# Other orders of Strassen's seven products in the MLP, and one sum of weights made from another sum's tile in SBUF

## Chip, core and metric

The program runs on one core of one Trainium2 chip. The metric is the device time of one execution in microseconds (us). TensorE is called PE here, VectorE DVE, ScalarE ACT, GpSimd POOL; SP is the engine that issues most of the plain DMAs. Weight loads into PE are listed apart as PEld.

## What is computed

One layer of a hybrid backbone on 1024 latent tokens of width 1024 (with 256 context tokens): a token mixer (long convolution, linear attention and a gated delta rule side by side, an input and an output projection), then a squared-ReLU MLP with a hidden width of 4096, and a final norm. The change touches the MLP alone:

```
def sq_relu_mlp(h, w1, w2):
    return jnp.square(jax.nn.relu(h @ w1)) @ w2

x = x + g1 * y                                    # y: output projection of the mixer
x = x + g2 * sq_relu_mlp(modulate(x, norm2_g[l], sh2, sc2), w_mlp1[l], w_mlp2[l])
return rmsnorm(x, final_norm_g)
```

All of it is float32.

## The kernel before

The recurrences of the mixer end near 900 us of the trace. Behind them come nine *stages*, one after the other: the output projection, and for each of four groups g of 1024 hidden channels an up stage (`in_w1[g]`) and a down stage (`in_w2[g]`). A stage multiplies a 1024x1024 block of weights by a 1024x1024 activation with one level of Strassen's scheme: seven products of 512x512 blocks, called product 1 to product 7 here, in an order that a tuple gives (`O1`, `O2`, `O3`). The up stage of g = 0 uses O2, the other up stages and all four down stages O1.

A product is four *chunks* p = 0 to 3. A chunk is 12 matmuls 128x512 into one bank of PSUM: four slices k of the contraction, each in three matmuls, because every float32 operand is split into two fp32r parts (`mm3`: hi x hi, hi x lo, lo x hi). So a product is 48 matmuls and a stage 336.

*Weights.* A product's weights are a sum of some of the four blocks (i, j) of the stage's weights (signs are already in the stored blocks). Such a sum lies in a tile `wr` of 128x2048 (1 MB). `PLANS[order]` has five such tiles, each a list in order of time: a pair (i, j) is a block to load or to add, a number is the product that then uses the tile. The first block of a tile is a plain load that SP issues (L1489); each further one is a DMA that adds to the tile, issued by POOL (L1483). There are four rooms of SBUF for the five tiles, so a tile's first load waits until the last user of the room's former tile is done. For each chunk the weights are split: ACT copies the high part (`S<-wr`, L291), then POOL subtracts to get the low part (`S<-wr,S`, L251). There are four buffers `S`, so the split can run four chunks, one product, ahead of PE.

*Activations.* `sums` makes the four operands `T` (slice k = 0 to 3) of the next product: perhaps a sum on DVE, then ACT's copy of the high part and DVE's subtraction (`T<-ar,T` in a down stage, `T<-h,T` in an up stage). There are ten buffers `T0` to `T9`.

*Results.* Products 6, 7 and 4 are added in PSUM on top of product 1's banks, and product 3 on top of product 5's (`bank`). After each chunk `take` reads the bank: in an up stage it makes the tiles `ar` of the squared ReLU, b11 and so on for the next down stage (b11 is done with product 2, b21 with product 4, b22 with 7 or 5, b12 with 3); in a down stage DVE adds it to the residual `x`.

Each engine runs its instructions in the order that a scheduler wrote at build time; an instruction that waits for a semaphore holds up all behind it on its engine. That holds for POOL's DMA issues, too: an adding DMA waits until the tile's former load or sum has landed. The up stage of g = 0 is special: its product 6 runs with its four chunks interleaved (`together`), so it needs all four `S` at once. The last stage splits product 4 in two halves of 256 columns, so that the final norm can start earlier.

Of the kernel before, what the change touches and what calls it, by code (L numbers as in the profile page):

```python
# [14 lines left out]
ADD, SUB, MUL, MIN, MAX = ALU.add, ALU.subtract, ALU.mult, ALU.min, ALU.max  # L15
# [163 lines left out]
def steps(st):  # L179
# [20 lines left out]
NORM1_AT = (1, 1)  # L200
FINAL_AT = (4, 1)

O1, O2, O3 = (1, 5, 6, 3, 2, 7, 4), (1, 2, 6, 7, 4, 5, 3), (1, 5, 2, 6, 7, 4, 3)

PLANS = {O1: (((0, 0), 1, (1, 0), 7), ((1, 0), (1, 1), 5, (0, 0), (0, 1), 3), ((1, 0), (1, 1), (0, 0), 6), ((0, 1), 2), ((1, 1), 4)),
         O2: (((0, 0), 1, (1, 0), 7), ((0, 1), 2), ((1, 0), (1, 1), (0, 0), 6, (0, 1), 3), ((1, 1), 4), ((1, 0), (1, 1), 5)),
         O3: (((0, 0), 1, (1, 0), 7), ((1, 0), (1, 1), 5, (0, 0), 6, (0, 1), 3), ((0, 1), 2), ((1, 1), 4))}
PAIRS = (0, 0, 0, 0, 1, 1, 1, 1)


class Build:
# [1257 lines left out]
    def weights(self, src, order):  # L1469

        gp = self.nc.gpsimd
        at, todo, tiles = {}, [list(t) for t in PLANS[order]], {}
        base = 8 * self.nS
        self.nS += 1

        def further(t):

            while todo[t] and not isinstance(todo[t][0], int):  # L1480
                i, j = todo[t].pop(0)
                if t in tiles:
                    gp.dma_start(tiles[t], src[:, i, j, :], accum_op=ADD)  # L1483
                else:
                    used = base + order.index([x for x in PLANS[order][t] if isinstance(x, int)][-1])
                    room = min(self.rooms, key=self.rooms.get)
                    self.rooms[room] = used
                    tiles[t] = (self.W if room < 2 else self.M).tile([128, 2048], F32, name=f"wr{room}", bufs=1)
                    self.nc.sync.dma_start(tiles[t], src[:, i, j, :])  # L1489
            if todo[t]:  # L1490
                at[todo[t].pop(0)] = t

        def begin(n):
            for t in sorted(range(5), key=lambda t: order.index(first(t))):
                if t < len(todo) and t not in tiles and order.index(first(t)) <= n:
                    further(t)

        def first(t):
            return next(x for x in PLANS[order][t] if isinstance(x, int)) if t < len(todo) else order[0]

        def get(i, p):
            return self.operand(self.W, "S", 4, tiles[at[i]][:, 512 * p:512 * p + 512], gp)
        return get, begin, lambda i: further(at[i])

    def stage(self, src, order, moving, take, after=None, last=None, first=None, together=()):
# [79 lines left out]
    def in_place(self, h, order):  # L1585

        def moving(i, k):
            b11, b12, b21, b22 = h(k, 0), h(k, 1), h(k + 4, 0), h(k + 4, 1)
            if order == O1:

                if i == 5:
                    self.tt(b11, b11, b12, SUB)
                elif i == 6:
                    self.minus(b11, b11, b22)
                elif i == 7:
                    self.tt(b12, b22, b12, SUB)
                elif i == 4:
                    self.minus(b21, b11, b21)
                return {1: b11, 5: b11, 6: b11, 3: b22, 2: b21, 7: b12, 4: b21}[i]

            if i == 5 and order == O3:
                t = self.temp()
                self.tt(t, b11, b12, SUB)
                return t
            if i == 6:
                self.tt(b12, b22, b12, SUB)
                self.minus(b11, b12, b11)
            elif i == 4:
                self.minus(b21, b11, b21)
            elif i == 5:  # L1610
                self.minus(b12, b11, b22)
            return {1: b11, 2: b21, 3: b22, 4: b21, 5: b12, 6: b11, 7: b12}[i]
        return moving
# [129 lines left out]
    def mlp(self):  # L1743
        nc, M, x1 = self.nc, self.M, self.x1
        h = lambda k, c: self.H[k][:, 512 * c:512 * c + 512]
        for g in range(4):
            order = O1 if g else O2
            b = {}
            new = lambda: M.tile([128, 512], F32, name="ar", bufs=16)

            def square(o, ps, sign):

                self.act(o, ps, AF.Relu, scale=sign)
                self.stt(o, ps, sign, o, MUL, MUL)

            def up(i, p, ps):
                n = p + 4
                at = {1: (p, 0), 6: (p, 1), 7: (n, 1), 4: (n, 0)}
                if order == O1:
                    at[5] = at.pop(7)  # L1760
                if i in at:
                    b[at[i]] = new()
                if i == 4:
                    square(b[n, 0], ps, -1.0)
                elif i in at:
                    nc.scalar.copy(b[at[i]], ps)
                elif i in (5, 7):
                    self.tt(b[n, 1], b[n, 1], ps, ADD)
                    self.act(b[n, 1], b[n, 1], AF.Relu, scale=-1.0)
                    self.act(b[n, 1], b[n, 1], AF.Square)  # L1770
                else:
                    o = b[p, 0] if i == 2 else b[p, 1]
                    self.tt(ps, o, ps, ADD)
                    square(o, ps, 1.0)
            self.stage(self.I["w1"][g], order, self.apart(h), up, *((*NORM1_AT, lambda: self.norm2(1)), None, None, (6,)) if g == 0 else ())
            acc = {} if g == 3 else None
            self.stage(self.I["w2"][g], O1, self.in_place(lambda k, c: b[k, c], O1), self.adder(40, acc), (*FINAL_AT, lambda: self.final(acc, 1)) if g == 3 else None,
                       (lambda s: self.final(acc, 0, s)) if g == 3 else None)


# [13 lines left out]
```

## Time and profile before

| | |
|---|---|
| median of 3 runs | 1669.11 us (1668.08 to 1672.71) |
| the profiled execution | 1667.06 us, its span 1665.3 us |
| PE busy | 1516.9 us, 91% of the span |
| DVE, ACT, POOL busy | 1264.2, 797.1, 704.3 us |
| matmuls of the nine stages (`psb<-T,S`) | 3072 |
| PE idle ahead of them | 25.7 us, of it 12.6 us ended by POOL's `S` |
| adding DMAs from `in_w` by POOL | 47 of 1 MB, 8.0 us from issue to landing |
| plain loads from `in_w` by SP | 40 of 1 MB, 5.5 us |

Idle time of an engine is told with the engine that ended it. A matmul's duration is longer than the interval from one matmul's start to the next, since they are pipelined; the interval is what counts for the time.

### The profile page before, as it was taken

To read this page: it belongs to the slowest core of one execution; us is meant where nothing else is said; L and a number is where in the kernel's file an instruction comes from. 1 tells how busy PE (TensorE), PEld (TensorE's weight loads), DVE (VectorE), ACT (ScalarE), POOL (GpSimd) and SP (SyncE) were. 2 spreads that over 40 slices of the span, in tenths; PEclk is the share of its full clock that TensorE was granted. 3 is DMA by queue.
4 is the path that set the end of the run, shared out by engine and by line. 5 is a ranking of instruction groups with operands and counts; after the bars stand their busy time and mean duration, and the time that the engine had idled before them with its cause. 6 is when DMAs were issued, how large, how long until landed. Compare 5 with 4: busy or idle time off the path is not lost.

```text
span 1665.3 us, 26163 instructions
## 1 busy us (share of the span) xinstructions
PE 1516.9 (91%) x10096; PEld 1217.1 (73%) x10096; DVE 1264.2 (76%) x1827; ACT 797.1 (48%) x1462; POOL 704.3 (42%) x509
## 2 busy tenths in 40 slices
PE   7799999989899988659798998989999999999997
PEld 2477877766688766558687787868878887787876
DVE  5954598896575586788987979797598769875986
ACT  5422223215765635535554455634564456445644
POOL 0311141413335221254833444655555555655544
PEclk9999999999999987769898999999999999999998
DMA  8333776747466610336438664555646666574632
GB/s 291 133 108 99 268 264 235 259 170 240 134 188 203 218 53 37 134 89 187 139 103 268 219 152 101 139 111 159 148 127 152 166 137 152 127 177 114 165 76 102
DMA packets 116452, 264.15 MB, mean 159 GB/s; under 512 B 29159, under 2 KB 74647, under 8 KB 101480
## 3 DMA queue, kind: packets, MB, share of 16 engines
q1 hardware_dynamic: 85800, 167.03, 29.1%
q0 software_dynamic: 11968, 75.50, 21.3%
q10 hardware_dynamic: 18560, 19.94, 4.0%
q8 instruction: 80, 1.31, 0.3%
q14 instruction: 44, 0.36, 0.1%
HBM read 220.69 MB, written 41.75 MB: 158 GB/s over the span
## 4 chain that ended last, share of the span: by engine, by line
PE 60%; DVE 18%; DMA 9%; issue 5%; ACT 5%; POOL 3%; ACTq 0%; POOLq 0%; SPq 0%; DVEq 0%
PE psb L223 45%; PE pss L223 8%; DMA wr<-in_w 5%; DVE lv L251 4%; POOL S L251 2%; PE psl L223 2%; DVE T L251 2%; DVE hb L251 2%; PE psi L223 1%; PE psd L223 1%; DVE bd L251 1%; DMA alo<-in_xT 1%; DVE acc L259 1%; ACT acc L263 1%; DMA dvt<-acc 1%
## 5 line engine op out<-in xcount | busy, mean ns | idle before, releaser
L223 PE MATMUL psb<-T,S 128*128 128x512 f32 (+1 forms) x3072 | 702.6, 390 | 25.7 <-POOL S L251 12.6
L223 PEld LDWEIGHTS psb<-T,S 128*128 128x128 f32 x3072 | 574.0, 190 | 152.9 <-POOL S L251 18.6
L251 POOL TENSOR_TENSOR S<-wr,S 128x512 fp32r<-128x512 f32 x252 | 367.7, 1507 | 262.0 <-ACT S L291 259.0
L291 ACT CAST S<-wr 128x512 fp32r<-128x512 f32 x252 | 154.3, 619 | 173.9 <-PE psb L223 95.9
L223 PE MATMUL psb<-ahi,wh 128*128 128x512 f32 x448 | 183.9, 412 | 7.9 <-ACT ahi L291 4.3
L223 PE MATMUL psb<-alo,wh 128*128 128x512 f32 x448 | 182.2, 407 | 0.0
L223 PE MATMUL psb<-ahi,wl 128*128 128x512 f32 x448 | 181.2, 405 | 0.0
L251 POOL TENSOR_TENSOR wl<-ws,wh 128x1024 fp32r<-128x1024 f32 x28 | 71.1, 2538 | 208.9 <-ACT wh L291 134.3
L259 DVE SCALAR_TENSOR_TENSOR acc<-psb,vecs,acc 128x504 f32<-128x504 f32 (+5 forms) x168 | 111.2, 677 | 50.0 <-ACT acc L263 47.7
L251 DVE TENSOR_TENSOR T<-ar,T 128x512 fp32r<-128x512 f32 x112 | 130.3, 1189 | 15.9 <-ACT T L291 15.9
L259 DVE SCALAR_TENSOR_TENSOR x<-psb,modT,x 128x512 f32<-128x512 f32 (+1 forms) x148 | 104.6, 726 | 39.5 <-PE psb L223 39.2
L251 DVE TENSOR_TENSOR T<-h,T 128x512 fp32r<-128x512 f32 x88 | 92.0, 1076 | 52.4 <-ACT T L291 52.1
L223 PEld LDWEIGHTS psb<-ahi,wh 128*128 128x128 f32 x448 | 87.7, 196 | 39.0 <-issue 9.1
L223 PEld LDWEIGHTS psb<-alo,wh 128*128 128x128 f32 x448 | 87.5, 195 | 25.8 <-issue 7.8
L223 PEld LDWEIGHTS psb<-ahi,wl 128*128 128x128 f32 x448 | 87.1, 194 | 22.3 <-issue 5.1
L291 ACT CAST T<-ar 128x512 fp32r<-128x512 f32 x112 | 67.7, 619 | 28.3 <-DVE ar L259 18.5
L1483 POOL DMA_DIRECT2D wr<-in_w x47 | 41.7, 888 | 80.8 <-DMA wr<-in_w 71.7
L251 POOL TENSOR_TENSOR bd<-lv,qT 64x1024 f32<-64x1024 f32 x16 | 50.1, 3135 | 37.7 <-PE pss L223 26.0
L263 ACT ACTIVATE acc<-psb,vecs 128x512 f32<-128x512 f32 (+1 forms) x48 | 31.1, 663 | 63.8 <-PE psb L223 31.6
L291 ACT CAST T<-h 128x512 fp32r<-128x512 f32 x88 | 52.3, 618 | 15.8 <-DVE h L259 11.4
L263 ACT ACTIVATE ar<-psb 128x512 f32<-128x512 f32 x48 | 28.7, 599 | 52.8 <-DVE psb L251 48.1
L263 ACT ACT_TABLE_LOAD x27 | 34.6, 1283 | 38.6 <-DVE acc L259 18.6
(334 smaller groups left out, 2662.6 us busy)
## 6 DMA issues: line engine op xcount, KB each, us to landing
wr<-in_w POOLq DMA_DIRECT2D x47, 1024.0 KB, 8.0
wr<-in_w SPq DMA_DIRECT2D x40, 1024.0 KB, 5.5
mw<-in_wmod SPq DMA_DIRECT2D x32, 512.0 KB, 5.6
ws<-in_win SPq DMA_DIRECT2D x28, 512.0 KB, 4.1
dft<-in_fw POOLq DMA_DIRECT2D x8, 1024.0 KB, 5.8
dft<-in_iv POOLq DMA_DIRECT2D x8, 1024.0 KB, 6.9
kq<-dKQ SPq DMA_DIRECT2D x64, 96.0 KB, 2.5
wl<-in_wmod SPq DMA_DIRECT2D x8, 512.0 KB, 4.1
```

Source lines behind the costliest of these rows:

```text
L223: return self.nc.tensor.matmul(out, lhsT=lhsT, rhs=rhs, start=start, stop=stop, skip_group_check=more)
L251: return (eng or self.nc.vector).tensor_tensor(out, a, b, op)
L259: return (eng or self.nc.vector).scalar_tensor_tensor(out, a, s, b, op0=op0, op1=op1)
L263: return self.nc.scalar.activation(out, a, f, bias=bias, scale=scale)
L291: self.nc.scalar.copy(hi, src)
L1483: gp.dma_start(tiles[t], src[:, i, j, :], accum_op=ADD)
```

## The change

Two orders are replaced or added, and the plans of O1 and O2 are new:

- O1 was 1, 5, 6, 3, 2, 7, 4 and is now 1, 5, 6, 7, 3, 2, 4.
- O4 = 1, 2, 5, 6, 7, 3, 4 is new and used by the down stage of g = 0 (before: O1).
- O2 keeps its order of products and O3 is as before.
- In the plans of O1, O2 and O4, product 5's sum (1,0)+(1,1) has a tile of its own, made by a load and one adding DMA. Product 6 needs (0,0)+(1,0)+(1,1): its tile is loaded with (0,0) and then gets product 5's whole tile added by a DMA from SBUF to SBUF (the entry `"1"`). Product 3's sum (all four blocks) is product 6's tile plus (0,1).

So an O1 stage has 4 adding DMAs (3 from HBM, 1 from SBUF) in place of 6, an O2 stage 4 in place of 5: 32 for the MLP in place of 47, 24 of them from HBM. The plain loads stay 40.

```
-O1, O2, O3 = (1, 5, 6, 3, 2, 7, 4), (1, 2, 6, 7, 4, 5, 3), (1, 5, 2, 6, 7, 4, 3)
-PLANS = {O1: (((0, 0), 1, (1, 0), 7), ((1, 0), (1, 1), 5, (0, 0), (0, 1), 3), ((1, 0), (1, 1), (0, 0), 6), ((0, 1), 2), ((1, 1), 4)),
-         O2: (((0, 0), 1, (1, 0), 7), ((0, 1), 2), ((1, 0), (1, 1), (0, 0), 6, (0, 1), 3), ((1, 1), 4), ((1, 0), (1, 1), 5)),
+O1, O2, O3, O4 = (1, 5, 6, 7, 3, 2, 4), (1, 2, 6, 7, 4, 5, 3), (1, 5, 2, 6, 7, 4, 3), (1, 2, 5, 6, 7, 3, 4)
+PLANS = {O1: (((0, 0), 1, (1, 0), 7), ((1, 0), (1, 1), 5), ((0, 0), "1", 6, (0, 1), 3), ((0, 1), 2), ((1, 1), 4)),
...
-                i, j = todo[t].pop(0)
+                what = todo[t].pop(0)
+                if isinstance(what, str):
+                    other = int(what)
+                    if other not in tiles:
+                        further(other)
+                    gp.dma_start(tiles[t], tiles[other], accum_op=ADD)
+                    continue
+                i, j = what
...
-            self.stage(self.I["w2"][g], O1, self.in_place(lambda k, c: b[k, c], O1), self.adder(40, acc), ...
+            down = O1 if g else O4
+            self.stage(self.I["w2"][g], down, self.in_place(lambda k, c: b[k, c], down), self.adder(40, acc), ...
```

The order of the instructions is the same up to the middle of the first up stage. Three places show what moves behind it.

POOL, from the last product of the up stage g = 1 (product 4, tile `wr_11168`) into the down stage g = 1 (`wr_11422` product 1, `wr_11436` product 5, `wr_11439` product 6), before:

```order
L1483 DMA wr_11439<-in_w 128x2048
L251 TENSOR_TENSOR S<-wr_11168,S 128x512
L1483 DMA wr_11439<-in_w 128x2048
L251 TENSOR_TENSOR S<-wr_11168,S 128x512
L251 TENSOR_TENSOR S<-wr_11422,S 128x512 x4
L1483 DMA wr_11422<-in_w 128x2048
L251 TENSOR_TENSOR S<-wr_11436,S 128x512 x4
L1483 DMA wr_11436<-in_w 128x2048
L251 TENSOR_TENSOR S<-wr_11439,S 128x512 x2
L1483 DMA wr_11436<-in_w 128x2048
L251 TENSOR_TENSOR S<-wr_11439,S 128x512 x2
L251 TENSOR_TENSOR S<-wr_11436,S 128x512 x4
```

The same place on POOL in the changed kernel (`wr_11163` product 4; then `wr_11417` product 1, `wr_11431` product 5, `wr_11434` product 6):

```order
L252 TENSOR_TENSOR S<-wr_11163,S 128x512 x2
L1487 DMA wr_11434<-wr_11431 128x2048
L252 TENSOR_TENSOR S<-wr_11163,S 128x512 x2
L252 TENSOR_TENSOR S<-wr_11417,S 128x512 x4
L1491 DMA wr_11417<-in_w 128x2048
L252 TENSOR_TENSOR S<-wr_11431,S 128x512 x4
L252 TENSOR_TENSOR S<-wr_11434,S 128x512 x4
L1491 DMA wr_11434<-in_w 128x2048
L252 TENSOR_TENSOR S<-wr_11417,S 128x512 x4
L252 TENSOR_TENSOR S<-wr_11434,S 128x512 x4
```

Before, twice two adding DMAs to one tile follow each other with one or two `S` between them (`wr_11439`, `wr_11436`), and the weights of product 3 (`wr_11436`) come right behind product 6's (`wr_11439`). Now no tile gets two additions so close, and product 7 (`wr_11417` again) stands between product 6 and product 3, both of which use `wr_11434`.

DVE, from the last product of the up stage g = 0 (product 3) towards the down stage g = 0, before (`ar_9866` is b12 of slice 0, `ar_9596` its b11, `T0_10274` product 5's first operand):

```order
L251 TENSOR_TENSOR psb_10061<-ar_9866,psb_10061 128x512
L259 SCALAR_TENSOR_TENSOR ar_9866<-psb_10061,ar_9866 128x512
L251 TENSOR_TENSOR ar_9596<-ar_9596,ar_9866 128x512
L251 TENSOR_TENSOR psb_10080<-ar_9868,psb_10080 128x512
L251 TENSOR_TENSOR ar_9866<-ar_9893,ar_9866 128x512
L251 TENSOR_TENSOR T0_10274<-ar_9596,T0_10274 128x512
```

The same place on DVE in the changed kernel (`T0_10270` and `T1_10273` are product 2's operands, `ar_9980` and `ar_9998` the b21 of slices 0 and 1; product 5's first operand is now `T4_10355`, further down):

```order
L252 TENSOR_TENSOR T0_10270<-ar_9980,T0_10270 128x512
L252 TENSOR_TENSOR T1_10273<-ar_9998,T1_10273 128x512
L252 TENSOR_TENSOR psb_10060<-ar_9868,psb_10060 128x512
L260 SCALAR_TENSOR_TENSOR ar_9868<-psb_10060,ar_9868 128x512
L252 TENSOR_TENSOR ar_9598<-ar_9598,ar_9868 128x512
L252 TENSOR_TENSOR psb_10079<-ar_9870,psb_10079 128x512
```

The second product of that down stage now takes operands that are ready before product 3 of the up stage is done; product 5, which needs the result of product 3, has become the third.

DVE, in the last product of the up stage g = 1, before (`T4_11430` and `T5_11433` are the last two operands of the down stage's product 1; `ar_10932` and its like are product 7's result):

```order
L251 TENSOR_TENSOR ar_10980<-ar_10980,psb_10882 128x512
L251 TENSOR_TENSOR ar_11036<-ar_10950,ar_11036 128x512
L251 TENSOR_TENSOR T4_11430<-ar_10895,T4_11430 128x512
L251 TENSOR_TENSOR ar_10895<-ar_10895,ar_11065 128x512
L251 TENSOR_TENSOR T5_11433<-ar_10913,T5_11433 128x512
L251 TENSOR_TENSOR ar_10998<-ar_10998,psb_10900 128x512
```

The same place in the changed kernel, where product 2 (`psb_11329` is its last chunk) is the last but one product and gives b11, the operand of the down stage's product 1 (`T4_11425`, `T5_11428`):

```order
L252 TENSOR_TENSOR psb_11329<-ar_10909,psb_11329 128x512
L252 TENSOR_TENSOR T6_11472<-ar_10827,T6_11472 128x512
L252 TENSOR_TENSOR ar_11028<-ar_10946,ar_11028 128x512
L252 TENSOR_TENSOR T4_11425<-ar_10891,T4_11425 128x512
L252 TENSOR_TENSOR T7_11476<-ar_10845,T7_11476 128x512
L260 SCALAR_TENSOR_TENSOR ar_10827<-ar_10827,ar_10928 128x512
L260 SCALAR_TENSOR_TENSOR ar_10909<-psb_11329,ar_10909 128x512
L260 SCALAR_TENSOR_TENSOR ar_11360<-psb_10814,ar_11360 128x512
L252 TENSOR_TENSOR ar_10891<-ar_10891,ar_11057 128x512
L260 SCALAR_TENSOR_TENSOR ar_10845<-ar_10845,ar_10946 128x512
L260 SCALAR_TENSOR_TENSOR ar_11378<-psb_10832,ar_11378 128x512
L252 TENSOR_TENSOR T5_11428<-ar_10909,T5_11428 128x512
```

Product 1's last operand stands twelve DVE rows behind the reading of product 2's last chunk; before, product 7 stood in between as a whole product.

## Rows read from the trace of the kernel before

**Rows 1.** Busy us of each engine per 100 us: PE, PEld, DVE, ACT, POOL, PEclk, DMA, GB/s.

```profile
1000.00:1100.00 100.00, 94.00 (x403) 76.29 (x402) 88.29 (x101) 56.99 (x106) 54.38 (x39) 0.97 0.53 125
1100.00:1200.00 100.00, 93.81 (x409) 76.63 (x410) 73.84 (x80) 45.92 (x80) 57.23 (x43) 1.00 0.61 138
...
1300.00:1400.00 100.00, 98.55 (x434) 80.83 (x433) 74.01 (x81) 50.80 (x91) 54.77 (x42) 1.00 0.60 149
```

**Rows 2.** Whom PE waited for, 900 to 1665 us: total, times, longest.

```profile
PE psb L223 <- POOL S L251: 12.6, 12, 3.5
PE psb L223 <- DVE T L251: 7.3, 3, 2.9
...
PE psb L223 <- ACT S L291: 4.0, 3, 2.3
...
PE psb L223 <- DVE ar L251: 1.6, 2, 0.8
```

**Rows 3.** PE's timeline: start, us, what, count, idle before and releaser.

```profile
1030.56 8.00 PE L223 MATMUL psb<-T,S 128*128 128x512 f32 x34 [0.73 <-POOL S L251]
1040.12 0.73 PE L223 MATMUL psb<-T,S 128*128 128x512 f32 x2 [1.57 <-ACT S L291]
1041.58 57.43 PE L223 MATMUL psb<-T,S 128*128 128x512 f32 x245 [0.72 <-POOL S L251]
1101.95 2.60 PE L223 MATMUL psb<-T,S 128*128 128x512 f32 x10 [2.94 <-DVE T L251]
1106.11 13.22 PE L223 MATMUL psb<-T,S 128*128 128x512 f32 x57 [1.55 <-DVE T L251]
1121.43 5.76 PE L223 MATMUL psb<-T,S 128*128 128x512 f32 x24 [2.10 <-POOL S L251]
1127.77 108.89 PE L223 MATMUL psb<-T,S 128*128 128x512 f32 x478 [0.58 <-POOL S L251]
1237.46 8.90 PE L223 MATMUL psb<-T,S 128*128 128x512 f32 x38 [0.81 <-DVE ar L251]
1249.82 113.51 PE L223 MATMUL psb<-T,S 128*128 128x512 f32 x492 [3.46 <-POOL S L251]
...
1407.75 30.22 PE L223 MATMUL psb<-T,S 128*128 128x512 f32 x132 [1.64 <-POOL S L251]
...
1601.72 1.05 PE L223 MATMUL psb<-T,S 128*128 128x512 f32 x2 [2.31 <-ACT S L291]
1603.08 38.70 PE L223 MATMUL psb<-T,S 128*128 128x512 f32 x185 [0.30 <-POOL S L251]
```

**Rows 4.** The granted clock (behind POOL's busy time) right after a stall and later.

```profile
1249.90:1253.50 3.60, 3.60 (x10) 2.86 (x11) 3.60 (x1) 1.85 (x3) 3.55 (x3) 0.57 0.89 184
1253.80:1257.40 3.60, 3.60 (x17) 2.97 (x16) 3.60 (x6) 2.22 (x4) 1.92 (x2) 1.00 0.93 337
```

**Rows 5.** POOL's timeline around the stall that ends at 1249.82.

```profile
1238.55 0.89 POOL L1483 DMA_DIRECT2D wr<-in_w  x1 [1.29 <-DMA wr<-in_w]
1240.45 1.29 POOL L251 TENSOR_TENSOR S<-wr,S 128x512 fp32r<-128x512 f32 x1 [1.01 <-ACT S L291]
1247.58 0.89 POOL L1483 DMA_DIRECT2D wr<-in_w  x1 [5.84 <-DMA wr<-in_w]
1248.19 5.26 POOL L251 TENSOR_TENSOR S<-wr,S 128x512 fp32r<-128x512 f32 x4
```

**Rows 6.** DMAs into `wr`: all from 980 us on, and POOL's, issue to landing.

```profile
DMA to landing us min/median/max: 4.6/8.0/9.5
...
wr<-in_w POOLq DMA_DIRECT2D x47, 1024.0 KB, 8.0
```

**Rows 7.** DVE's timeline in the same stall; and all `T<-ar` (busy, mean ns).

```profile
1247.15 0.68 DVE L259 SCALAR_TENSOR_TENSOR ar<-psb,ar 128x512 f32<-128x512 f32 x1
1247.75 6.27 DVE L251 TENSOR_TENSOR ar<-ar 128x512 f32<-128x512 f32 x1
...
L251 DVE TENSOR_TENSOR T<-ar,T 128x512 fp32r<-128x512 f32 x112 | 130.3, 1189 | 15.9 <-ACT T L291 15.9
```

More of the change, by code (lines that the diff above doesn't have):

```diff
@@ L201 @@
 FINAL_AT = (4, 1)
-O1, O2, O3 = (1, 5, 6, 3, 2, 7, 4), (1, 2, 6, 7, 4, 5, 3), (1, 5, 2, 6, 7, 4, 3)
-PLANS = {O1: (((0, 0), 1, (1, 0), 7), ((1, 0), (1, 1), 5, (0, 0), (0, 1), 3), ((1, 0), (1, 1), (0, 0), 6), ((0, 1), 2), ((1, 1), 4)),
-         O2: (((0, 0), 1, (1, 0), 7), ((0, 1), 2), ((1, 0), (1, 1), (0, 0), 6, (0, 1), 3), ((1, 1), 4), ((1, 0), (1, 1), 5)),
-         O3: (((0, 0), 1, (1, 0), 7), ((1, 0), (1, 1), 5, (0, 0), 6, (0, 1), 3), ((0, 1), 2), ((1, 1), 4))}
+O1, O2, O3, O4 = (1, 5, 6, 7, 3, 2, 4), (1, 2, 6, 7, 4, 5, 3), (1, 5, 2, 6, 7, 4, 3), (1, 2, 5, 6, 7, 3, 4)
+PLANS = {O1: (((0, 0), 1, (1, 0), 7), ((1, 0), (1, 1), 5), ((0, 0), "1", 6, (0, 1), 3), ((0, 1), 2), ((1, 1), 4)),
+         O2: (((0, 0), 1, (1, 0), 7), ((1, 0), (1, 1), 5), ((0, 0), "1", 6, (0, 1), 3), ((0, 1), 2), ((1, 1), 4)),
+         O3: (((0, 0), 1, (1, 0), 7), ((1, 0), (1, 1), 5, (0, 0), 6, (0, 1), 3), ((0, 1), 2), ((1, 1), 4)),
+         O4: (((0, 0), 1, (1, 0), 7), ((1, 0), (1, 1), 5), ((0, 0), "1", 6, (0, 1), 3), ((0, 1), 2), ((1, 1), 4))}
 PAIRS = (0, 0, 0, 0, 1, 1, 1, 1)
@@ L1588, in moving @@
             b11, b12, b21, b22 = h(k, 0), h(k, 1), h(k + 4, 0), h(k + 4, 1)
-            if order == O1:
+            if order in (O1, O4):
                 if i == 5:
@@ L1758, in up @@
                 at = {1: (p, 0), 6: (p, 1), 7: (n, 1), 4: (n, 0)}
-                if order == O1:
+                if order in (O1, O4):
                     at[5] = at.pop(7)
@@ L1776, in mlp @@
             acc = {} if g == 3 else None
-            self.stage(self.I["w2"][g], O1, self.in_place(lambda k, c: b[k, c], O1), self.adder(40, acc), (*FINAL_AT, lambda: self.final(acc, 1)) if g == 3 else None,
+            down = O1 if g else O4
+            self.stage(self.I["w2"][g], down, self.in_place(lambda k, c: b[k, c], down), self.adder(40, acc), (*FINAL_AT, lambda: self.final(acc, 1)) if g == 3 else None,
                        (lambda s: self.final(acc, 0, s)) if g == 3 else None)
```

## Prediction

> **What bounds the kernel now.** Read first how busy PE is per 100 us. In the MLP it is 94.0% busy from 1000 to 1100 us and 98.6% from 1300 to 1400, while DVE is at 74 to 88% and POOL near 55% [rows 1]. So PE sets the end, and a change that leaves its matmuls alone can only win back PE's idle time. The second view says who ended that idle time: POOL's split of weights 12.6 us in 12 stalls, DVE's operands `T` 7.3 us in 3, ACT's copy of weights 4.0 us in 3, DVE's `ar` 1.6 us in 2 [rows 2]. The third, PE's timeline, says where [rows 3].
>
> What can be had at most comes from counting. From 1127.77 on PE runs 478 matmuls in 108.89 us without a break [rows 3]: 0.2278 us each, 48 of them (a product) 10.9 us. From 1041.58 to 1641.78 (the end of the last row of rows 3) are 46 + 51 x 48 = 2494 full matmuls and 43 of half width: 46 left of product 7 of the first up stage, 51 products, and the start of the last one. At 0.2278 and half of it they need 568.1 + 4.9 = 573.0 us; they took 600.2. So 27.2 us are lost there, in stalls and in what follows them.
>
> What follows them is the clock. After the stall of 3.46 us the granted clock is 0.57 for 3.6 us, in which 10 matmuls start, and 1.00 in the next 3.6 us, in which 17 do [rows 4]: the lower level (1.2 GHz) for most of the first stretch, then 2.4 GHz. The row that holds it has 113.51 us for 492 matmuls, 1.4 us over the pace; the row from 1603.08 is 1.4 us over too (142 full and 43 half), the one from 1041.58 1.6 us [rows 3].
>
> Why POOL is late is in its own timeline. At 1238.55 it issues the adding DMA of block (1,0) to product 6's tile, at 1247.58 that of (1,1), after 5.84 us idle for the first to land; four `S` then follow without a pause, the first of which is product 4's last chunk [rows 5], and PE resumes at 1249.82 [rows 3]. So the pattern is: two additions to one tile in a row, 8.0 us each [rows 6], with a split behind the wait. It stands twice in each O1 stage, ahead of product 6 and of product 3.
>
> **The change part by part.** *DMAs.* 15 adding issues of 0.89 us [rows 5] leave POOL's queue, 13.4 us of an engine that is 55% busy: nothing by itself. What counts is that no tile now gets two additions so close. Product 5's tile gets its (1,1), then four splits run, then the new DMA adds it to product 6's tile. Splits keep PE's pace of 2.73 us a chunk, so the four take 10.9 us, and the landing takes 8.0 (9.5 at most) [rows 6]: no wait, or a short one. If it does wait, a split has room: its buffer is free three chunks (8.2 us) before PE needs it, ACT's and POOL's work is about 2.1 us (0.6, and 1.3 to 1.5 in rows 5), so a hold under 6.1 us costs PE nothing. Product 3's weights now need one addition, with product 7 in between: from product 6's last split to product 3's first deadline are over 16 us for a DMA of 8.
>
> *The SBUF to SBUF addition.* No row has one. The nearest are a plain load, 4.6 us, and an addition from HBM, 8.0 [rows 6]; at worst I let it take twice that, 16. It is issued in the last but one product of the former stage and is needed about three and a half products (38 us) later, so all three values cost nothing; I take 8.0, since it too reads two streams and writes one.
>
> *What goes.* All 12 stalls on POOL but the one at 1041.58 (product 6 there runs with its chunks interleaved, so product 7's first split must come late; the 1.57 us on ACT at 1040.12 stays for that reason): 11.9 us. Of ACT's, 4.0 - 1.57 = 2.4. The two stalls on `T` at 1101.95 and 1106.11, 4.5 us: product 5 of the first down stage needs product 3 of the up stage, which was two products before it and is now three. The two on `ar`, 1.6: product 7's result must be read before product 4 adds to the same bank, and 7 no longer stands right before 4. Together 20.4 us idle. With half clock and restart the whole loss goes: 27.2 - 1.6 (behind 1041.58, stays) + 0.7 (1030.56, before the stretch) = 26.3 us.
>
> *What comes.* First, product 7 now follows 6 in the same bank, so PE waits until 6's chunk is read; there are three chunks, 8.2 us, for it. The same neighbourhood cost 0.8 us twice in eight stages. Bounds 0 and 5.6 (0.8 in all seven), I take 0.5. Second, an up stage's product 2 is now the last but one, and its result is the operand of the next product 1. Behind the reading of its last chunk stand 12 DVE rows to that operand, 4 of them `T` at 1.19 us and 8 near 0.68 [rows 7]: 10.2 us, against 10.9 us of product 4 and 2.0 of product 1's first nine matmuls. 2.7 us are spare, and a DVE operation took 6.27 in place of 0.68 us while POOL's four splits ran on end [rows 5, 7]. Bounds for each of the three boundaries: 0, and 4.5 + 0.3 = 4.8 us (what the first boundary costs now, two restarts with it). I take 1.0 each, nearer to nothing, as POOL's bursts go with the waits. Third, in the first up stage the splits of product 6 are no longer held, but its own operands are late by little: 0.5 of the 0.7 stays. Around the end (final norm) the same operations run; 0.
>
> Sum: 26.3 - 0.5 - 3.0 - 0.5 = 22.3 us. Against the profiled execution, 1667.06 - 22.3 = 1644.8. The median is 2.05 above that execution, so 1646.9, say 1647.
>
> **Rivals.** *DVE takes over (1658).* All three boundaries stall as the first one does now, 14.4 us, and the banks of 6 and 7 cost 1.0: 1667.06 - 26.3 + 14.4 + 1.0 = 1656.2, 1658 with the offset. For it: DVE is 88% busy around the first boundary [rows 1], and its order has become denser ahead of each down stage. Against: the work is the same and the rows were just as many in the two products before. The row behind it is the 6.27 us. The Trainium skill (SBUF — State Buffer, Who interferes with whom) says why such rows occur: a DVE instruction with two SBUF inputs shares a read interface with GpSimd, and whoever starts first keeps it for the whole instruction. By that rule the 6.27 us agree with four splits in a row, evenly spread splits would hold DVE by about one split at a time, and the boundaries would cost nearer 0 than 4.8 each; but since DVE and POOL both run dense there, it keeps this rival alive.
>
> *The wait moves to the new DMA (1683, slower).* The DMA `wr<-wr` on POOL waits for product 5's tile to land, and product 4's last two splits stand behind it, in every stage from the first down stage on. If landing takes over 10.9 + 6.1 = 17 us from issue, PE stalls there as it did at 1249.82: 3.46 + 1.4 + 0.2 = 5.1 us, seven times 35.7, and 1667.06 - 26.3 + 4.0 + 35.7 = 1680.5, 1683 with the offset. Against: the longest landing is 9.5, and there is less traffic than before.
>
> *It does not do what it says (1666).* POOL is late for its own work rather than for landings, and only the stalls on `T` and `ar` go: 6.1 + 0.8 (four restarts) - 4.0 = 2.9 us, 1664.2, 1666 with the offset. Against: 108.89 us at full pace with as many splits per product.
>
> **How the numbers follow.** Forecast 0.74, DVE 0.13, no effect 0.07, slower 0.06. A measurement of this kernel tells about 0.3% (5 us) from no change, so the first two are faster (0.87), the third is the same (0.07), the fourth slower (0.06). The range: nothing given back would be 1643; 3 us more for the uncertain count of lost time and runs that differ by as much, 1639 below; above it takes in the DVE rival and some of its bounds, 1662.
>
> **What would show it.** Right: PE's waits on POOL's splits fall from 12.6 to under 2 us, those on `T` in the first down stage are gone, the intervals between stalls grow beyond 113 us, POOL's idle time before its adding DMAs falls, and DVE's operations over 3 us disappear. DVE's `T` or `ar` as PE's releaser at the starts of the later down stages would be the DVE rival; POOL's `wr<-wr` with an idle time over 6 us before it and a split behind it would be the slower one. The prediction is wrong if the additions from SBUF take much over 17 us, or if PE loses its time to an engine that rows 2 do not name.

## The result, and the profile after

The changed kernel takes 1641.63 us (median of 4 runs, 1638.78 to 1647.01), beside it the kernel before 1670.91: ratio 0.9833 (95% interval 0.9808 to 0.9858). Forecast was 1647, in a range of 1639 to 1662. The profiled execution is one of 1638.78 us, span 1637.0.

PE's waits from 900 us on (total, times, longest) answer to [rows 2], and PE's timeline to [rows 3]:

```profile
PE psb L224 <- DVE T L252: 3.4, 3, 3.0
...
PE psb L224 <- DVE x L260: 1.1, 2, 0.9
PE psb L224 <- ACT S L292: 1.1, 1, 1.1
PE psb L224 <- POOL S L252: 1.1, 2, 0.7
```

```profile
1037.90 0.73 PE L224 MATMUL psb<-T,S 128*128 128x512 f32 x2 [1.10 <-ACT S L292]
1039.36 65.12 PE L224 MATMUL psb<-T,S 128*128 128x512 f32 x286 [0.73 <-POOL S L252]
1105.39 133.32 PE L224 MATMUL psb<-T,S 128*128 128x512 f32 x586 [0.91 <-DVE x L260]
1238.93 152.72 PE L224 MATMUL psb<-T,S 128*128 128x512 f32 x672 [0.21 <-DVE T L252]
1391.87 159.07 PE L224 MATMUL psb<-T,S 128*128 128x512 f32 x700 [0.22 <-DVE T L252]
1551.29 59.88 PE L224 MATMUL psb<-T,S 128*128 128x512 f32 x274 [0.35 <-POOL S L252]
```

Of 12.6 us of waiting for POOL's `S`, 1.1 are left, and from 1105 us on PE stops only three times, for 0.2 to 0.4 us each, up to the final norm. (3.0 of the 3.4 us on `T` stand in the output projection, ahead of the MLP; 2.8 of the 7.3 stood there before.) POOL's own waits for landings ahead of adding DMAs, from 980 us on, in the kernel before and then in the changed one:

```profile
POOL wr L1483 <- DMA wr<-in_w: 71.7, 21, 5.8
```

```profile
POOL wr L1487 <- DMA wr<-in_w: 9.4, 6, 4.3
...
POOL wr L1491 <- DMA wr<-in_w: 4.0, 2, 2.7
```

The new kind of addition, in the page's list of DMA issues (count, size, us to landing), costs what was put in for it (8.0):

```profile
wr<-in_w POOLq DMA_DIRECT2D x24, 1024.0 KB, 8.0
wr<-wr POOLq DMA_DIRECT2D x8, 1024.0 KB, 7.4
```

To compare traces stage by stage, take the start of each stage's first matmul (336 apart). At full pace a stage lasts 76.2 us, the value that three stages of the changed kernel share; what is above it is *lost*. This leaves out the recurrences, in which executions of one and the same program differ: the up stage g = 0 begins between 994 and 1007 us in the traces below. Lost us, from PE's rows; w1 is an up stage, w2 a down stage, 0 to 3 the group, and 3.0 us of the final norm are taken out of the last:

| kernel | w1,0: product 1 | w1,0: 6 and 7 | w2,0 | w1,1 | w2,1 | w1,2 | w2,2 | w1,3 | w2,3 | sum from w2,0 |
|---|---|---|---|---|---|---|---|---|---|---|
| before | 5.8 | 5.5 | 8.4 | 6.7 | 0.0 | 4.0 | 1.8 | 1.4 | 5.5 | 27.8 |
| after | 5.4 | 2.5 | 1.4 | 0.0 | 0.6 | 0.0 | 0.6 | 0.0 | 0.7 | 3.3 |
| after, again | 12.0 | 3.6 | 1.5 | 0.0 | 1.6 | 0.0 | 0.6 | 0.0 | 0.0 | 3.7 |
| orders only | 5.8 | 5.5 | 3.7 | 0.0 | 3.2 | 0.0 | 3.4 | 0.0 | 1.5 | 11.7 |
| plans only | 11.7 | 3.5 | 5.2 | 2.9 | 2.4 | 3.4 | 2.3 | 1.8 | 3.2 | 21.3 |
| sum from HBM | 5.8 | 5.4 | 4.3 | 0.0 | 2.8 | 0.0 | 1.0 | 0.0 | 0.0 | 8.1 |
| no O4 | 11.8 | 3.4 | 3.2 | 0.0 | 0.6 | 0.0 | 0.7 | 0.0 | 0.0 | 4.4 |
| added thrice | 6.5 | 4.4 | 4.7 | 0.0 | 0.6 | 0.0 | 0.7 | 0.0 | 0.0 | 6.0 |
| O2's old plan | 5.6 | 5.4 | 1.5 | 0.0 | 0.6 | 0.0 | 0.6 | 0.0 | 1.6 | 4.3 |
| up stages in O4 | 11.5 | 3.7 | 1.5 | 0.0 | 0.0 | 0.0 | 0.0 | 0.0 | 0.0 | 1.5 |
| no interleaving | 10.5 | 0.1 | 7.6 | 0.0 | 0.6 | 0.0 | 0.6 | 0.0 | 0.0 | 8.8 |
| up O4, O2's old plan | 5.8 | 5.6 | 1.4 | 0.0 | 0.0 | 0.0 | 0.0 | 0.0 | 0.0 | 1.5 |
| the same, no interleaving | 5.8 | 1.1 | 6.5 | 0.0 | 0.0 | 0.0 | 0.0 | 0.0 | 0.0 | 6.5 |
| orders only, one input | 5.4 | 2.2 | 1.0 | 0.0 | 0.0 | 0.0 | 0.0 | 0.0 | 0.0 | 1.0 |

Between the two profiled executions, 24.5 us (27.8 - 3.3) come from the first down stage on, 3.4 from the first up stage, 0.4 from ahead of it: 28.3, the difference of the spans.

Most of the medians below lie between 1646 and 1650 us, and the changed kernel's own two are 1641.63 and, in its second run below, 1648.84. So where a variant differs from the changed kernel by a few us, the reading rests on the rows of one profiled execution each, not on the times.

### The profile page after: what moved, and what is told of

Read it like the earlier page. It is cut to its first block, busy times and chain, and to the rows that moved or that the text cites. A ratio compares the mean times of both kernels' runs of the same rounds, so it can differ in the third digit from the quotient of the medians.

```text
span 1637.0 us, 26134 instructions
## 1 busy us (share of the span) xinstructions
PE 1509.1 (92%) x10096; PEld 1215.9 (74%) x10096; DVE 1236.8 (76%) x1827; ACT 803.0 (49%) x1462; POOL 694.8 (42%) x494
## 4 chain that ended last, share of the span: by engine, by line
PE 62%; DVE 22%; ACT 5%; DMA 5%; issue 4%; POOL 2%; SPq 0%; POOLq 0%; ACTq 0%; DVEq 0%
PE psb L224 47%; PE pss L224 8%; DVE lv L252 4%; DVE T L252 3%; PE psl L224 2%; DVE ar L260 2%; DVE hb L252 2%; DVE ar L252 1%; PE psi L224 1%; PE psd L224 1%; DVE acc L260 1%; DVE bd L252 1%; DMA dft<-in_fw 1%; DVE psb L252 1%; DMA alo<-in_xT 1%
## 5 line engine op out<-in xcount | busy, mean ns | idle before, releaser
L224 PE MATMUL psb<-T,S 128*128 128x512 f32 (+1 forms) x3072 | 693.7, 387 | 6.7 <-DVE T L252 3.4
L252 DVE TENSOR_TENSOR T<-h,T 128x512 fp32r<-128x512 f32 x88 | 86.2, 1010 | 46.1 <-ACT T L292 44.8
L252 DVE TENSOR_TENSOR T<-ar,T 128x512 fp32r<-128x512 f32 x112 | 111.7, 1024 | 6.2 <-ACT T L292 5.9
L224 PEld LDWEIGHTS psb<-ahi,wl 128*128 128x128 f32 x448 | 87.1, 194 | 22.3 <-issue 5.1
L1774 ACT COPY ar<-psb 128x512 f32<-128x512 f32 x48 | 28.2, 587 | 49.8 <-PE psb L224 49.3
L292 ACT CAST wh<-ws 128x1024 fp32r<-128x1024 f32 x28 | 29.3, 1045 | 44.4 <-PE psb L224 35.1
```

What stands on the lines that cost most here:

```text
L224: return self.nc.tensor.matmul(out, lhsT=lhsT, rhs=rhs, start=start, stop=stop, skip_group_check=more)
L252: return (eng or self.nc.vector).tensor_tensor(out, a, b, op)
L292: self.nc.scalar.copy(hi, src)
```

## Experiments: is it the orders or the plans?

**The new orders with the old plans.** Product 6's tile again gets two additions from HBM, product 3's too.

```
-PLANS = {O1: (((0, 0), 1, (1, 0), 7), ((1, 0), (1, 1), 5), ((0, 0), "1", 6, (0, 1), 3), ((0, 1), 2), ((1, 1), 4)),
+PLANS = {O1: (((0, 0), 1, (1, 0), 7), ((1, 0), (1, 1), 5, (0, 0), (0, 1), 3), ((1, 0), (1, 1), (0, 0), 6), ((0, 1), 2), ((1, 1), 4)),
```

> The new orders of products with the plans of the kernel before: all 47 additions come from HBM, and product 6's tile again gets two in a row, now with two splits between them. Theory A (two additions to one tile in a row hold POOL, whatever the order): the stalls that product 6's pair caused before (5.4, 2.0 and 0.95 us in the last product of the second and third up stage and at the start of the last down stage, 8.4 in all) stay, and so do 3.0 us in the first up stage; 1641.6 + 11.4 = 1653 us. Theory B (the order alone is enough: with product 7 between 6 and 3 and two splits, 5.5 us, between the two additions of 8.0 us each, POOL waits 2.5 to 3.4 us, under the 6.1 us of room that a split has): only the first up stage loses, 1645 us, and POOL idles 2 to 4 us ahead of each second addition without a stall of PE behind it.

Measured: 1651.82 us, ratio 0.9908 (0.9878 to 0.9937). The time is that of theory A, but the rows say that neither theory is right. POOL waits, as A wants, and PE hardly waits for its splits, as B wants (0.44 and 0.62 us from the first down stage on). PE waits for DVE. POOL, DVE and PE in the second down stage (start, length, idle before and its releaser):

```profile
1264.75 0.89 POOL L1491 DMA_DIRECT2D wr<-in_w  x1 [0.30 <-POOL S L252]
1265.36 2.84 POOL L252 TENSOR_TENSOR S<-wr,S 128x512 fp32r<-128x512 f32 x2
1273.31 0.89 POOL L1491 DMA_DIRECT2D wr<-in_w  x1 [5.11 <-DMA wr<-in_w]
1273.92 6.57 POOL L252 TENSOR_TENSOR S<-wr,S 128x512 fp32r<-128x512 f32 x5
```

```profile
1273.73 0.74 DVE L260 SCALAR_TENSOR_TENSOR x<-psb,modT,x 128x512 f32<-128x512 f32 x1
1274.39 7.26 DVE L252 TENSOR_TENSOR T<-ar,T 128x512 fp32r<-128x512 f32 x2
1281.58 2.05 DVE L260 SCALAR_TENSOR_TENSOR x<-psb,modT,x 128x512 f32<-128x512 f32 x3
```

```profile
1282.46 122.23 PE L224 MATMUL psb<-T,S 128*128 128x512 f32 x538 [1.56 <-DVE x L260]
```

POOL idles 5.11 us for the first of two additions; five splits have piled up behind it and run in one go, 6.57 us. Two `T` of DVE that met them take 7.26 us in place of 1.3. The `x` behind them, which reads product 6's bank, is late, and product 7 waits for that bank. So a wait of POOL that stays within a split's room is still paid for, by DVE.

**The new plans with the old orders.**

```
-O1, O2, O3, O4 = (1, 5, 6, 7, 3, 2, 4), ...
+O1, O2, O3, O4 = (1, 5, 6, 3, 2, 7, 4), ...
-            down = O1 if g else O4
+            down = O1
```

> The new plans (product 6's sum from product 5's tile in SBUF, 32 additions) with the order of before, product 3 right behind product 6 and the first down stage in O1. Theory A (order is what counts): product 3's tile now gets its only addition after product 6's last split, 0.9 + 8.0 us, and its split takes 2.1 more, so product 3 starts 11.0 + 2.1 - 10.9 = 2.2 us late, with a restart 2.7, in seven O1 stages, 19 us; the two stalls on T in the first down stage (5.1) and the two on ar (1.9) are back: 1641.6 + 26 = 1667 us. Theory C (the sum in SBUF is the gain, since POOL issues and waits for fewer additions): only T and ar are back, 1649 us.

Measured: 1668.88 us, ratio 0.9998 (0.9977 to 1.0018). The time is that of theory A: fewer additions by themselves bring nothing there. The rows are less simple. From the first down stage on 21.3 us are lost, 6.5 less than before, but the first up stage loses 3.9 more (11.7 + 3.5 for 5.8 + 5.5), which A did not have in its sum. What A argued is there, smaller than it was put: product 3 starts late in each O1 stage, for ACT's copy of a tile that lands too late, and loses more a little later, for DVE; product 4 waits for `ar` again:

```profile
1248.27 43.76 PE L224 MATMUL psb<-T,S 128*128 128x512 f32 x192 [0.79 <-DVE ar L252]
1292.57 11.32 PE L224 MATMUL psb<-T,S 128*128 128x512 f32 x48 [0.54 <-ACT S L292]
1305.02 65.56 PE L224 MATMUL psb<-T,S 128*128 128x512 f32 x288 [1.12 <-DVE x L260]
```

Product 3's late start was put at 2.2 us each and is 0.7 to 1.5; with the waits on `x` and `ar` a stage from the second up stage on loses 1.8 to 3.4.

**The changed kernel, product 6's blocks from HBM.** The smallest edit that takes the new addition away: `((0, 0), "1", 6, ...)` becomes `((0, 0), (1, 0), (1, 1), 6, ...)`.

> The changed kernel, but product 6's tile gets (1,0) and (1,1) from HBM in place of product 5's tile from SBUF: 40 additions, a pair in a row for each product 6. Theory A (pairs hold POOL): the 8.4 us of product 6's pairs are back, 1650 us. Theory B (a pair with two splits between it fits into a split's room of 6.1 us): 1642 to 1645 us, POOL idle 2 to 4 us ahead of the second addition, PE at full pace behind it.

Measured: 1647.59 us, ratio 0.9877 (0.9854 to 0.9900). In the trace 8.1 us are lost from the first down stage on, where the changed kernel loses 3.3, and 3.3 more in the first up stage. The stalls are again DVE's (1114.19 first down stage, 1251.19 the start of the second):

```profile
1114.19 134.51 PE L224 MATMUL psb<-T,S 128*128 128x512 f32 x586 [2.57 <-DVE x L260]
1251.19 152.66 PE L224 MATMUL psb<-T,S 128*128 128x512 f32 x672 [2.48 <-DVE T L252]
```

Of 24.5 us from the first down stage on, then, the orders alone give 16.1 (27.8 - 11.7), the plans alone 6.5 (27.8 - 21.3); the two together give 24.5.

**Is DVE held by POOL's splits, and is that the stall?** The orders-only kernel once more, with DVE writing the low part of `T` as a copy:

```
-        self.split(t[:, 0], t[:, 1], src, le=le)
+        if le is None:
+            self.nc.scalar.copy(t[:, 0], src)
+            self.nc.vector.tensor_copy(t[:, 1], t[:, 0].bitcast(F32))
+        else:
+            self.split(t[:, 0], t[:, 1], src, le=le)
```

> The new orders with the old plans (the run with orders only), but DVE writes the low part of T as a copy of the high part, one input from SBUF in place of two (so the output isn't the reference's; nothing else is left out). With two inputs, rows of DVE that met a run of POOL's splits took 3.8 us (two splits), 5.1 (three) and 6.3 to 6.7 (four and five), and PE then waited for DVE's x behind them, 3.4, 1.6 and 1.6 us. Theory A (an operation of DVE with two inputs from SBUF is held until POOL's run of splits is over, and that is the stall): rows that write T stay under 1 us even beside four splits, the stalls on x in the down stages go, and the nine stages lose 6 to 9 us less; rows of ar with two inputs are still held (4 to 5 us). Theory B (any operation of DVE is held by POOL's run, or PE's wait for x has another cause): rows that write T still take 4 to 6 us, the stalls on x stay.

Measured: 1634.86 us, ratio 0.9807 (0.9784 to 0.9829). From the first down stage on 1.0 us is lost in place of 11.7, and PE runs to the final norm in one piece:

```profile
1111.45 488.75 PE L224 MATMUL psb<-T,S 128*128 128x512 f32 x2155 [0.75 <-ACT S L292]
```

So the stalls of the orders-only kernel were DVE's lateness: that half of theory A stands. Its other half, that an instruction with one input is not held, fell. DVE's copies are held by POOL's splits, too. POOL's three splits from 1248.86, and two of DVE's copies, one beside them and one alone:

```profile
1248.86 4.10 POOL L252 TENSOR_TENSOR S<-wr,S 128x512 fp32r<-128x512 f32 x3
```

```profile
1248.77 4.49 DVE L1466 CAST T<-T 128x512 fp32r<-128x512 f32 x1
...
1263.39 0.43 DVE L1466 CAST T<-T 128x512 fp32r<-128x512 f32 x1 [0.25 <-ACT T L1465]
```

What is not held is the `x` that reads one operand from PSUM and one from SBUF: 116 such rows from 1050 us on in this trace, and in those of before, after and orders only, and none is longer than 0.76 us. The copy takes 0.43 us alone where the subtraction takes 0.68, which leaves DVE more time between the runs of splits. The Trainium skill (SBUF — State Buffer, Who interferes with whom) names both kinds of instruction that share an interface with GpSimd, those with two inputs in SBUF and copies in a mode with two ports. The held rows agree with it; in which mode these copies ran no row tells. The experiment was meant to take the shared interface away and only shortened the instruction. So that POOL's splits are what made DVE late is read from the rows that stand beside each other; no run here takes the hold away and leaves all else.

## Experiments: O4, the price of the sum, the first up stage

**The first down stage in O1** (`down = O1` for all g, the rest as changed).

> The changed kernel with the first down stage in O1, so that its product 5, which needs product 3 of the first up stage, is the second product again. Theory A (distance alone): the two stalls on T there (2.94 and 1.55 us, with restarts 5.1) are back and the 1.3 us that products 2 and 5 lose there now go: 1641.6 + 3.8 = 1645.4 us. Theory B (part of that lateness was DVE held by POOL's splits in a row, which stay away): product 5 loses only the 2.2 us that it loses with the new plans alone: 1642.5 us.

Measured: 1649.74 us, ratio 0.9877 (0.9856 to 0.9898); the total holds another effect (product 1 of the first up stage, below), the rows decide. The stage loses 3.2 us in place of 1.4, by two waits on `T`:

```profile
1104.21 2.60 PE L224 MATMUL psb<-T,S 128*128 128x512 f32 x10 [0.96 <-DVE T L252]
1108.37 140.19 PE L224 MATMUL psb<-T,S 128*128 128x512 f32 x617 [1.55 <-DVE T L252]
```

Between the theories, nearer to B: of the 2.94 us that product 5 waited before [rows 3], 2.0 went without O4. O4 is worth 1.8 us.

**Product 5's tile added three times**, `"1", "1", "1"`.

> The changed kernel with product 5's tile added three times to product 6's tile (so the output isn't the reference's): the sum from SBUF costs three landings of 7.4 us, 22 us from the first issue. If the addition from SBUF has the room that the forecast gave it (38 us to its first use, and splits between the issues), little changes: POOL waits under 2 us ahead of the second and third, 1642 to 1645 us. By the forecast's rival (landing over 17 us after the issue stalls PE by 5.1 us in each of seven stages) it is 1641.6 + 35.7 = 1677 us.

Measured: 1646.88 us, ratio 0.9864 (0.9840 to 0.9887). In the stages from the second up stage on nothing changes for PE (1.3 us lost, the changed kernel 1.9): 22 us of landing fit there, though POOL waits up to 4.4 us ahead of the second and third addition, not under 2. The loss grows ahead of that: in products 2, 6 and 7 of the first up stage, where the first use is near, 2.1 + 1.9 us more, and in the first down stage, 3.3 more. There the third addition, issued at 1102.65 after 3.99 us of waiting, has four splits right behind it, and two `T` of DVE beside them take 6.28 us:

```profile
1103.26 5.33 POOL L252 TENSOR_TENSOR S<-wr,S 128x512 fp32r<-128x512 f32 x4
```

```profile
1103.47 6.28 DVE L252 TENSOR_TENSOR T<-ar,T 128x512 fp32r<-128x512 f32 x2
```

PE then waits 2.82 us for DVE's `x`. The rival by which a late sum stalls PE in seven stages is out by far.

**The first up stage with its old plan** (O2's plan as before, the rest as changed).

> The changed kernel with the plan of the first up stage (O2) as before. The forecast gave that stage 0.2 us; it gained 3.4. If the plan did it (product 6's fourth split was behind a wait for an addition, and the half clock followed the longer idle time), products 6 and 7 take 2.7 us each over their pace again and the granted clock behind the stall is near 0.58 again: 1645 us. If it came from elsewhere, products 6 and 7 stay at 1.3 and 1.1 and the time at 1642 us.

Measured: 1646.29 us, ratio 0.9876 (0.9844 to 0.9908). Products 6 and 7 lose 5.4 us again: the plan did it. The old plan holds product 6's fourth split, PE waits three times there (0.65, 1.53 and 0.73 us), and the granted clock behind the last of them is 0.53, the lower of its two levels for most of the stretch; with the new plan PE waits twice in the same place (1.10 and 0.73 us) and goes on at 1.00. Granted clock is the last but two of these columns, first this kernel, then the changed one:

```profile
1046.30:1049.90 3.60, 3.60 (x9) 2.91 (x10) 3.60 (x4) 3.01 (x6) 3.04 (x2) 0.53 0.00 0
```

```profile
1039.40:1043.00 3.60, 3.60 (x16) 2.99 (x17) 3.60 (x4) 3.60 (x8) 3.04 (x2) 1.00 0.00 0
```

**The changed kernel once more.** Four variants with O2's new plan lost 10.5 to 11.8 us in product 1 of the first up stage, though their instructions up to there come in the changed kernel's order.

> The changed kernel itself once more, beside the two kernels below. Product 1 of the first up stage, whose instructions come in the same order in all kernels with the new plan of O2, took 5.3 us over its pace in the changed kernel's profile and 10.5 to 11.7 in four variants. Theory A (one place with two outcomes: an operand T of DVE starts just before or just after POOL's splits, and is held by them in the second case): executions of this kernel spread by 6 us or more, and a profile shows one of the two values, 5 to 6 or 10 to 12. Theory B (a difference of the variants): 5.3 again, and the time at 0.983 of the kernel before.

Measured: 1648.84 us, ratio 0.9844 (0.9821 to 0.9867). Theory A: this time the same kernel loses 12.0 us there (the *long way* from here on; the short one is 5.4). DVE, which makes the sums `acc` that PE waits for, and POOL beside it, first in the profile above and then in this one, with PE's wait:

```profile
1001.32 1.28 DVE L252 TENSOR_TENSOR T<-h,T 128x512 fp32r<-128x512 f32 x2
...
1001.99 3.45 POOL L252 TENSOR_TENSOR S<-wr,S 128x512 fp32r<-128x512 f32 x2
```

```profile
1007.04 4.09 DVE L252 TENSOR_TENSOR T<-h,T 128x512 fp32r<-128x512 f32 x2
...
1011.65 3.16 DVE L252 TENSOR_TENSOR T<-h,T 128x512 fp32r<-128x512 f32 x1
...
1007.74 2.83 POOL L252 TENSOR_TENSOR S<-wr,S 128x512 fp32r<-128x512 f32 x2
...
1015.56 1.84 PE L224 MATMUL psb<-ones,acc 128*128 128x1 f32 x8 [5.72 <-DVE acc L252]
```

The two splits behind `wr<-wr` start 0.67 us after the pair of `T` in the one, 0.70 in the other. In the first DVE's second `T` goes ahead and POOL's splits are stretched (3.45 us); in the second the splits take 2.83 and DVE's pair 4.09, and the next `T` is held by the next two splits. The two starts differ by 0.03 us and the outcomes by 6.6 us, and 1.1 us more in product 6. What decides between them the recorded starts don't tell: DVE's second `T` begins ahead of the splits in both.

The spread of the times is not this place alone. Of the 12.9 us between the two profiled executions of the changed kernel, 7.7 come from the first up stage and 5.7 from ahead of it (it begins at 998.55 and at 1004.24 us).

Four profiles with O2's new plan that took the long way lose 15.2 to 15.6 us in products 1, 6 and 7 together (a fifth, without interleaving, 10.6), the one that did not 7.9 (10.9 with the sum added thrice), and those with product 6's sum from HBM or the old plan 11.0 to 11.4 wherever product 6 is interleaved (7.6 in the run with one input). In these profiles, then, that part of the change wins 3.4 us by the short way and loses about 4 by the long one, which came five times in seven.

**The up stages g = 1 to 3 in O4**, so that product 2 stands second.

```
-            order = O1 if g else O2
+            order = O4 if g else O2
```

> The changed kernel with the up stages g = 1 to 3 in O4 (1, 2, 5, 6, 7, 3, 4), so that product 2, which gives product 1 of the down stage its operand, stands second and not last but one. The 0.6 us that product 1 loses at three boundaries (1.8 in all) should go. If nothing else turns late: 1640 us. If product 5, whose banks are then those of product 2, waits for DVE to read them as in the first down stage (0.9 to 1.3 us each): 1643 us, with DVE as the releaser at product 5's start.

Measured: 1648.35 us, ratio 0.9862 (0.9826 to 0.9897), with the long way in product 1 of the profiled execution (which is the fastest of the four all the same, 1639.44: its first up stage begins at 994.02 us). In the rows the boundaries' 0.6 us are gone, nothing takes their place, and PE runs from the first down stage to the final norm without a stop:

```profile
1108.22 491.97 PE L224 MATMUL psb<-T,S 128*128 128x512 f32 x2168 [0.93 <-DVE x L260]
```

**Product 6 of the first up stage without interleaved chunks** (`(6,)` becomes `()`).

> The changed kernel without the interleaving of product 6's chunks in the first up stage. If the interleaving is what makes product 7's split late (its four S are free only when product 6 ends), the 2.4 us that products 6 and 7 lose there go. In their place the first chunk waits for product 6's last operand, which is done 3.3 us after the product's start and needed 2.05 us after it: 1.3 us. Together 1.1 us less: 1640.5 us. If the operand's lateness costs a second stall or half clock behind it: 1644 us.

Measured: 1648.14 us, ratio 0.9856 (0.9812 to 0.9900). Products 6 and 7 lose 0.1 us, better than expected, and the first down stage 7.6 in place of 1.4: PE waits 4.5 us there for DVE's `x`.

**Both better parts: up stages in O4, O2's old plan; and the same without interleaving.**

> The changed kernel with the up stages g = 1 to 3 in O4 and the old plan for the first up stage. Product 1 of the first up stage should lose 5.6 us in each execution, products 6 and 7 5.4, the three boundaries nothing: against the changed kernel's profile 3.0 - 1.8 = 1.2 us more; against an execution of it in which product 1 loses 11.5, 4.9 us less. If the second is the usual case (theory A of the run beside it), this kernel is the faster of the two by 2 to 4 us.

> The same, and product 6 of the first up stage without interleaving its chunks, which left 0 of the 2.4 us of products 6 and 7 with the new plan. If the old plan's sum is there in time, 5.4 us less than the run before, 1637 us; but products 2 and 5 of the first down stage lost 7.5 us in place of 1.4 without the interleaving (DVE late with reading banks), and if that follows from the interleaving and not from chance, the two cancel and the time is that of the run before.

Measured, beside the changed kernel's second run: 1643.07 us, ratio 0.9812 (0.9788 to 0.9836), and 1642.37 us, 0.9814 (0.9787 to 0.9841), against 0.9844 (0.9821 to 0.9867). By the medians the first is 5.8 us faster than the changed kernel in this comparison; the intervals overlap, and the changed kernel's first median, 1641.63, is 1.4 below it. So neither is shown to be faster. Product 1 loses 5.8 in both. Without interleaving the first down stage loses 6.5, as it lost 7.6 in the other run without it, and that cancels the gain; why DVE is later there without it was not tested.

## Why the prediction was right, and where its sum was off

The forecast took 22.3 us off the profiled execution; the profiles differ by 28.3. Step by step:

- **What bounds, and what goes.** Right: PE's matmuls bound the stages, and nearly all of the loss between them goes. The count of the loss was too small. It rested on 0.2278 us a matmul, from 108.89 us for 478 [rows 3]; the unbroken row of 2168 above gives 491.97 / 2168 = 0.2269, and over 2494 matmuls the difference is 2.2 us of loss not seen. The row's length takes in the last matmul's own 0.39 us and 0.38 us of intervals that are longer than the rest, and the division spreads both over the count; a row of thousands, or the distance of two matmuls' starts (76.2 us for the 336 of a stage), is the better measure.
- **POOL's pairs of additions.** The pattern was right: with the sum from HBM, two additions in a row again, 4.8 us from the first down stage on are lost again. But the sentence that a hold under 6.1 us costs PE nothing was wrong in its scope. POOL's splits were in time; the run of splits behind the hold held DVE. The forecast had this row (6.27 us, [rows 7]) and used it only for the boundaries. Runs of three splits or more right behind a DMA issue, with a DVE instruction beside them that can be held, number 7 in the trace of before, 9 with the orders only, 9 with the sum from HBM and 3 in the changed kernel (from 1000 us on): here the plans help.
- **The stalls on `T` in the first down stage.** Put down to the distance between products 3 and 5 alone, 4.5 us and restarts. The run without O4 shows that 5.2 of the 8.4 us go without it. In exchange O4 brought a wait that the forecast didn't have: product 5 takes the banks of product 2, and waits 0.9 us for DVE's `x`; 1.4 us in that stage.
- **The first up stage.** 0.2 us were expected, 3.0 came in products 6 and 7, by the new plan and the clock that no longer falls. In other executions product 1 takes 6.6 back. The forecast treated this stage's start as untouched; that the new addition is issued in product 1, with two splits behind it, was in the order of POOL's instructions.
- **The boundaries.** 1.0 each was taken. The first two of the three cost 0.6 each, and the run with O4 in the up stages shows that it is product 2's place, as was argued. The third cost nothing: the 0.7 of the last stage is a wait on POOL's split (0.35 us, at 1551.29), which four other profiles with the same orders and plans in that stage don't have (a fifth has a longer one, 0.68 us).
- **Banks of 6 and 7.** 0.5 was taken, nothing came.
- **The sum in SBUF.** 8.0 us was taken, 7.0 to 8.6 measured; three in a row cost PE nothing from the second up stage on.

So 22.3 + 2.2 (pace) + 2.8 (first up stage) + 0.8 (product 1 and the start, 0.4 each) + 1.8 (boundaries) - 0.7 (POOL's split in the last stage) + 0.5 (banks) - 1.4 (first down stage) = 28.3. The second run of the changed kernel, 1648.84, has the other outcome in product 1; the forecast of 1647 lies between the two medians. That it lies so close to the second is luck: the forecast had neither this outcome nor the loss that it saw too small.

Of the signs named, PE's waits on POOL's splits (1.1 us), the stalls on `T`, the longer stretches and POOL's idle time came as told. One did not: DVE's operations over 3 us have not disappeared. From 1000 us on there are 10 such rows in the trace of before and 3 in the changed kernel's, the longest 5.07 us, each beside three splits right behind a DMA issue.

Of the rivals, the one without effect is out by PE's waits on POOL's splits, 12.6 us before and 1.1 after; the slower one is excluded by the sum added thrice; the one in which DVE takes over is not what happened, but its mechanism is what makes the old plans cost time in the new orders.

## What to carry to other kernels

A DMA issue that waits in POOL's queue does its harm twice: what stands right behind it is late, and then runs in one go and keeps DVE out. Look for DVE rows several times their usual length and lay POOL's rows beside them before reading a wait on DVE as work of DVE. Reordering paid here where it put another product between an addition and its use; fewer additions without that gave nothing in the time (0.9998). And take one profile twice before a gain of a few us is put down to an edit: here one place has two outcomes 6.6 us apart, and the work ahead of it ends up to 13 us apart (994 to 1007 us).

## What the runs showed that was not expected

A DVE instruction with two inputs in SBUF that meets a run of POOL's splits right behind a DMA issue of POOL is held until the last of the run is done, not by one of them: 3.75 us beside two, 5.08 beside three, 6.27 beside four ([rows 5, 7]), 1.2 to 1.3 us more for each further split. DVE and POOL in the trace of before (two splits):

```profile
1591.67 3.75 DVE L251 TENSOR_TENSOR T<-ar,T 128x512 fp32r<-128x512 f32 x1
...
1592.04 2.83 POOL L251 TENSOR_TENSOR S<-wr,S 128x512 fp32r<-128x512 f32 x2
```

and in the last of the variants, up stages in O4 without interleaving (three):

```profile
1245.87 5.08 DVE L252 TENSOR_TENSOR T<-ar,T 128x512 fp32r<-128x512 f32 x1
...
1246.31 4.08 POOL L252 TENSOR_TENSOR S<-wr,S 128x512 fp32r<-128x512 f32 x3
```

A run without a pause doesn't do this by itself. In the changed kernel four splits that stand behind a wait on ACT, with no DMA issue just ahead, take turns with DVE, and four `T` beside them take 1.1 to 1.8 us each (here two and two):

```profile
1252.71 6.41 POOL L252 TENSOR_TENSOR S<-wr,S 128x512 fp32r<-128x512 f32 x4 [2.39 <-ACT S L292]
```

```profile
1253.38 2.87 DVE L252 TENSOR_TENSOR T<-ar,T 128x512 fp32r<-128x512 f32 x2
...
1256.84 2.83 DVE L252 TENSOR_TENSOR T<-ar,T 128x512 fp32r<-128x512 f32 x2
```

The fourteen traces together say the same. Take the runs of three splits or more, from 1000 us on, that have a DVE instruction of the kinds that are held beside them, begun before the last split: 63 stand right behind a DMA issue, and in 61 of these DVE is held to the end of the run; 81 do not, and the longest DVE row beside them is 1.87 us.

The Trainium skill (SBUF — State Buffer, Who interferes with whom) says that whoever issues first has the shared pair for the whole instruction. The runs without an issue ahead agree, with DVE held by about one split at a time. Those right behind an issue go further: the run counts as one, and in the two pairs of rows shown first the DVE instruction, which began 0.4 us ahead of the first split, came last all the same. Why the issue makes the difference was not tested.
